# Tying weight sums two steps back, and moving a spilled operand's stores to another DMA queue, in a one-core hybrid decoder layer

## The chip, the cores and the metric

The kernel runs on one core of a Trainium2 chip. The metric is the device time of one execution in microseconds, median of several runs. Engines are named as the profile names them: PE is the matrix engine (TensorE), PEld its weight loads, DVE is VectorE, ACT is ScalarE, POOL is GpSimd, SP is SyncE, which here only issues DMAs. Each engine takes its instructions in order and waits at an instruction until the semaphores it names are reached.

## The reference

One decoder layer over 1040 positions (16 learned tokens and 1024 of input), width 1024, everything in float32:

```
u = rmsnorm(h);  z = u @ w_in            -> q, k, v, x_rec, y_rec
A = gelu(y_rec) * rg_lru(conv4(x_rec));  B = sliding-window attention with sinks
h = h + rmsnorm(concat(B, A) @ w_out)
h = h + rmsnorm(square(relu(rmsnorm(h) @ w_ff1)) @ w_ff2)
```

The change lies in the last line, the feed-forward part: a product of 1024x1024 by 1024x4096 and one of 1024x4096 by 4096x1024.

## The kernel before

Products of float32 are made of three matmuls of float32r: each operand is split into a high part (a copy with a cast to float32r, on ACT, line 96) and a low part (source minus high part, on DVE, line 99), and `mm3` (lines 125, 126, 127) adds high x high, high x low and low x high into one bank. Where the text says "low part" of a weight tile it means the line-99 subtraction.

Both feed-forward products are done by a scheme of Strassen's kind: the matrices are cut in two by two blocks, and seven products of sums of blocks replace eight. That makes sums: `combine` (line 989) is one DVE addition or subtraction, and some sums of weight blocks are left to the DMA engines (`accum_op=ADD`, line 1258, from POOL's queue: the first block is loaded by SP, and the second is added to it in place).

**First product.** One of the sums of the activations, T4, is needed late. Its two operand pairs (high and low part of each half of the contraction) are made early in `t_rest` (from line 1163), stored to `t4_dram` by four DMAs of 512 KB (line 1165; the trace calls it t_dram), and read back into `ot4` by four DMAs some 130 us later (line 1217). Four other tiles of weight sums per round are kept the same way: `prep_a` stores each to `s_dram` (line 1034, POOL's queue), and the tile that it leaves is refilled by a weight load. `product` runs through four blocks of the contraction, three matmuls each; the first of the products with T4 is written otherwise, in `product_by_parts`: four matmuls of high x high, then four of low weight x high operand, then four of high weight x low operand, so that T4's low parts are needed last.

**Second product.** A list of 56 steps, seven products (i) times eight pieces (q) of the contraction, at 24 matmuls a step. `fetch_2(n)` loads the weight block or blocks of step n into the two `raw` and two `e` buffers, `prep_2(n)` sums them where a sum is DVE's, splits them into one of four `ws` buffers, and makes the activation side. In products 1 and 2 (steps 8 to 23) the sum of two weight blocks is an accumulating DMA where q % 3 < 2, and a DVE `combine` in steps 10, 13, 18 and 21; in products 3, 4 and 6 it is DVE's more often. A `raw` or `e` buffer is free for a later step's load when its low part or its `combine` is done.

The order of each engine's instructions is not that of the source. A scheduler with a timeline model places them, and `behind(name, ins)` adds a constraint to it without a semaphore: `ins` goes behind the named instruction. In the last product (i == 6) the weight sum is held behind the low part of the step before:

```
ins = combine(raws[0], raws[0], raws[1], wx[2])
if i == 6:
    behind(w_low[0], ins)
```

Of the kernel before, what the change touches and what calls it, by code (L numbers as in the profile page):

```python
# [37 lines left out]
def hybrid_layer(  # L38
# [6 lines left out]
    nc = tc.nc  # L45
# [12 lines left out]
    def slot(tag, shape, dt=F32):  # L58
        uid[0] += 1
        return slab.tile(shape, dt, tag=tag, name=f"{tag}{uid[0]}", bufs=bufs[tag])  # L60

    def pair(tag, shape):
        return slot(tag, shape, F32R), slot(tag, shape, F32R)

    def bank(tag, shape=(P, 512)):
        uid[0] += 1
        return ps.tile(list(shape), F32, tag=tag, name=f"ps_{tag}{uid[0]}")

    def f32(ap):
        return ap.bitcast(F32)  # L70
# [23 lines left out]
    def split(hi, lo, src, eng=None):  # L94
        if eng is None:
            nc.scalar.copy(hi, src)  # L96
        else:
            eng.tensor_copy(hi, src)
        low = nc.vector.tensor_tensor(lo, src, f32(hi), op=ALU.subtract).ins  # L99
        mark[0] = low.name  # L100
        return low
# [4 lines left out]
    def behind(name, *inss):  # L106
        for ins in inss:
            tc.add_manual_dep(
                ins, name,
                mybir.DependencyInfo(  # L110
                    mybir.DependencyClass.NoSync, mybir.DependencyReason.DATA
                ),
                reason="order",
            )
# [8 lines left out]
    def mm3(dst, lhs, rhs, start, stop):  # L123
        (lh, ll), (rh, rl) = lhs, rhs
        nc.tensor.matmul(dst, lh, rh, start=start, stop=False, skip_group_check=True)  # L125
        nc.tensor.matmul(dst, lh, rl, start=False, stop=False, skip_group_check=True)  # L126
        last_mm[0] = nc.tensor.matmul(  # L127
            dst, ll, rh, start=False, stop=stop, skip_group_check=True
        ).ins.name
# [363 lines left out]
    for b in range(4):  # L493
# [3 lines left out]
        if b == 0:  # L497

            acc = [bank("acc"), bank("acc")]
# [11 lines left out]
            for w, (t0, n), sink, tag in (  # L511
                (wq, (16, 256), sink_q0, "o"), (wx, piece, sink_x0, "acc"),
            ):
                acc = bank(tag)
# [395 lines left out]
    t4_dram = dpool.tile([P, 2, 4, 512], F32, name="t4_dram")  # L910
# [77 lines left out]
    def combine(dst, x0, x1, op):  # L988
        return nc.vector.tensor_tensor(dst, x0, x1, op=op).ins  # L989
# [9 lines left out]
    def product(acc, w, op, first):  # L999
        wh, wl = w  # L1000
        for kc in range(4):
            hh, ll = op[kc // 2]
            mm3(
                acc, (wh[:, kc, :], wl[:, kc, :]), (hh[:, kc % 2, :], ll[:, kc % 2, :]),
                first and kc == 0, kc == 3,
            )
# [50 lines left out]
    def fetch_c(p):  # L1057
        r1 = slot(("e", "raw")[third.index(p) % 2], [P, 4, 256])
        w1_load(r1, 1, p, 0, 2)
        return r1  # L1060

    def prep_c(p):
        r1 = raw_c.pop(p)
        hi, lo = pair("ws", [P, 4, 256])
        split(hi, lo, r1)
        return (hi[:, :, LO], lo[:, :, LO]), (hi[:, :, HI], lo[:, :, HI])
# [8 lines left out]
    def block(k, p):  # L1075
        q = p // 2
        if fb[k][q] is None:
            fb[k][q] = slot(FTAG[k][q], [P, 2, 512])
        return fb[k][q][:, p % 2, :]

    def activate(k, q):
        t_ = fb[k][q]
        nc.scalar.activation(t_, t_, AF.Relu)
        return nc.scalar.activation(t_, t_, AF.Square).ins
# [20 lines left out]
    for t in range(8):  # L1105
# [12 lines left out]
        if t == 6:  # L1118
            b21 = operand(u2f[0][2:4])
            hl = slot("b", ESH, F32R), slot("e", ESH, F32R)  # L1120
# [33 lines left out]
    def t_rest(k):  # L1154
        i = k % 2
        if k < 2:
            behind(mark[0], combine(u2f[1][i], u2f[1][i], u2f[0][i], ALU.subtract))
        elif k < 4:
            behind(mark[0], combine(t2[i], u2f[0][2 + i], t2[i], ALU.subtract))
        else:  # L1160
            hl = pair("a", [P, 2, 512])
            late = mark[0]
            behind(late, split(*hl, t2[i]))
            for n in range(2):
                nc.sync.dma_start(t4_dram[:, n, 2 * i : 2 * i + 2, :], f32(hl[n]))

    raw_b, raw_c = {}, {}
    for p in range(16):
        if p + 2 < 16:
            wa[p + 2] = prep_a(p + 2, None if p else urgent)  # L1170
        if p >= 13:
            raw_b[p - 13] = fetch_b(p - 13)
        product(ya[p], wa[p][1], ot2, False)
        nc.scalar.copy(block("12", p), ya[p])
        if 4 <= p + 2 < 16:
            p1(p + 2, wa[p + 2][0])
        product(ya[p], wa[p][2], ot3, False)
        nc.scalar.copy(block("21", p), ya[p])
        if 3 <= p < 9:
            t_rest(p - 3)  # L1180

        if p == 14:
            ot1 = operand(u2f[1][0:2])
# [13 lines left out]
    for p in range(16):  # L1197
# [7 lines left out]
        if p == 15:  # L1205
            wc = {third[0]: prep_c(third[0])}
# [5 lines left out]
        if p == 2:  # L1212
            ob21 = operand(u2f[0][2:4])
    ot4 = [pair("b", [P, 2, 512]) for _ in range(2)]
    for n in range(2):
        for i in range(2):
            nc.sync.dma_start(f32(ot4[i][n]), t4_dram[:, n, 2 * i : 2 * i + 2, :])

    def product_by_parts(acc, w, op):
        for k, (a, b) in enumerate(((0, 0), (1, 0), (0, 1))):  # L1220
            for kc in range(4):
                nc.tensor.matmul(
                    acc, w[a][:, kc, :], op[kc // 2][b][:, kc % 2, :],
                    start=k == 0 and kc == 0, stop=k == 2 and kc == 3,
                    skip_group_check=True,
                )

# [19 lines left out]
    def fetch_2(n):  # L1249
        i, q = steps[n]  # L1250
        wx = PLAN[i][1]
        tags = (("raw", "e"), ("e", "raw"))[n % 2] if i < 6 else LASTW[q]
        raws = []
        for (a, b), tag in zip(wx[:2], tags):
            if len(wx) == 3 and wx[2] is ADD and raws and (
                q % 3 < 2 if i < 6 else tag is None
            ):
                nc.gpsimd.dma_start(raws[0], w2v[q, a, b], accum_op=ADD)
                break
            r = slot(tag, [P, 2, 512])  # L1260
            nc.sync.dma_start(r, w2v[q, a, b])
            raws.append(r)
        return raws

    def prep_2(n, tag="ws"):
        i, q = steps[n]
        fx, wx, _ = PLAN[i]
        raws = raw_2.pop(n)
        if len(raws) == 2:
            ins = combine(raws[0], raws[0], raws[1], wx[2])  # L1270
            if i == 6:
                behind(w_low[0], ins)
        wh, wl = pair(tag, [P, 2, 512])
        w_low[0] = split(wh, wl, raws[0]).name
        if len(fx) == 3:
            f = slot("b", [P, 2, 512])
            combine(f, fb[fx[0]][q], fb[fx[1]][q], fx[2])
        else:
            f = fb[fx[0]][q]
        fh, fl = pair("b", [P, 2, 512])  # L1280
        split(fh, fl, f)
        return fh, fl, wh, wl
# [2 lines left out]
    steps = [(i, q) for i in range(7) for q in range(8)]  # L1285
    ready, raw_2 = {}, {}

    w_low = [None]

    load_root(squared)  # L1290

# [2 lines left out]
    for n, p in enumerate(third):  # L1294
        if n + 2 < 16:
            raw_c[third[n + 2]] = fetch_c(third[n + 2])
        if n >= 13:
            raw_2[n - 13] = fetch_2(n - 13)
        if n + 1 < 16:
            wc[third[n + 1]] = prep_c(third[n + 1])  # L1300
        if n == 15:
            ready[0] = prep_2(0)
        if p not in a12_early:
            y2 = bank(("acc", "s")[p % 2])
            product(y2, wc[p][0], ob21, True)
            nc.vector.tensor_tensor(block("11", p), y2, block("11", p), op=ALU.add)
        y4 = bank(("pt", "o")[p % 2])
        if n == 0:
            product_by_parts(y4, wc[p][1], ot4)
        else:  # L1310
            product(y4, wc[p][1], ot4, True)
        nc.vector.tensor_tensor(block("21", p), y4, block("21", p), op=ALU.add)
        done.add(p)
        if p ^ 1 in done:
            activate("11", p // 2)
            activate("21", p // 2)
# [183 lines left out]
```

## Time and profile before

| | us |
|---|---|
| median of 3 runs | 957.42 (956.74 to 957.98) |
| the profiled execution, own time | 957.43 |
| its span in the trace | 955.7 |
| PE busy in the span | 944.6 |
| DVE, ACT, POOL busy | 659.3, 504.3, 124.6 |

The span is counted from the first to the last instruction of the trace; 1.7 us of the execution lie outside it. A line of a timeline has start and length in us, engine, source line, operation and tiles, how many were merged, and in brackets how long the engine sat idle before it and what ended that. Buffer numbers are left out, so which step a `raw`, `e` or `ws` belongs to is told in the text. A line of the waits has total time, number of times and the longest. The granted TensorE clock is 1.0 throughout. Loads and casts that are named below by step were put to their steps by the order of the instructions in the built program.

### The profile page before, as it was taken

Reading aid. Unit: us, or ns where it says so; the run is one execution under the profiler, and the core shown is the slowest. Engines: PE = TensorE matmul, PEld = TensorE weight load, DVE = VectorE, ACT = ScalarE, POOL = GpSimd, SP = SyncE. Lnnn points to the kernel's source line nnn. Section 1 sums busy time; section 2 is a strip of 40 time slices with the busy share of each in tenths; the row PEclk is TensorE's granted clock in tenths of the full one; section 3 lists DMA queues with packets and bytes.
Section 4 is the critical chain, followed back from the end, with each engine's and each line's share of the span. In section 5 each row is a group of like instructions: output and inputs, shape, how many; then the busy total and the mean of one; then the engine's idle time right before and its main releaser. Section 6 shows DMA issues by size and latency. Waiting matters only on the chain.

```text
span 955.7 us, 12406 instructions
## 1 busy us (share of the span) xinstructions
PE 944.6 (99%) x4728; PEld 789.8 (83%) x4728; DVE 659.3 (69%) x845; ACT 504.3 (53%) x854; POOL 124.6 (13%) x184
## 2 busy tenths in 40 slices
PE   9999999999999999999999999999999999999996
PEld 8999999877888877888888878888888788888885
DVE  6567997779866776665644465476576776779883
ACT  7537766478645554443555575563433343446441
POOL 4102563420020100000000000000111100001201
PEclk9999999999999999999999999999999999999999
DMA  8221011104235466675522353324767765547934
GB/s 271 57 67 23 24 45 46 45 23 134 77 120 177 133 220 198 197 259 160 184 102 90 110 192 119 109 92 129 176 171 182 198 219 178 197 133 199 241 67 89
DMA packets 88200, 130.22 MB, mean 136 GB/s; under 512 B 13702, under 2 KB 52630, under 8 KB 88140
## 3 DMA queue, kind: packets, MB, share of 16 engines
q1 hardware_dynamic: 79548, 106.54, 34.3%
q0 software_dynamic: 8160, 21.57, 10.9%
q10 hardware_dynamic: 432, 1.31, 0.4%
q8 instruction: 37, 0.61, 0.3%
q14 instruction: 23, 0.19, 0.1%
HBM read 109.93 MB, written 18.87 MB: 135 GB/s over the span
## 4 chain that ended last, share of the span: by engine, by line
PE 91%; DVE 3%; ACT 2%; SPq 1%; POOL 1%; DMA 1%; issue 1%; DVEq 0%; ACTq 0%; POOLq 0%
PE ps_acc L125 11%; PE ps_acc L126 11%; PE ps_acc L127 11%; PE ps_pt L125 7%; PE ps_pt L126 7%; PE ps_pt L127 6%; PE ps_s L127 6%; PE ps_s L126 6%; PE ps_s L125 6%; PE ps_o L127 5%; PE ps_o L126 5%; PE ps_o L125 5%; PE ps_o L684 1%; POOL c L673 1%; ACT c L82 1%; DMA c<-in_x_dram 1%
## 5 line engine op out<-in xcount | busy, mean ns | idle before, releaser
L96 ACT CAST ws<-raw 128x1024 fp32r<-128x1024 f32 (+1 forms) x68 | 69.6, 1024 | 121.6 <-PE ps_o L126 46.9
L99 DVE TENSOR_TENSOR ws<-raw,ws 128x1024 fp32r<-128x1024 f32 (+1 forms) x69 | 82.4, 1195 | 53.8 <-ACT ws L96 52.8
L125 PE MATMUL ps_acc<-a,ws 128*128 128x256 f32 (+2 forms) x256 | 85.8, 335 | 0.0
L127 PE MATMUL ps_acc<-a,ws 128*128 128x256 f32 (+2 forms) x256 | 85.2, 333 | 0.0
L126 PE MATMUL ps_acc<-a,ws 128*128 128x256 f32 (+2 forms) x256 | 85.1, 333 | 0.0
L99 DVE TENSOR_TENSOR b<-b,b 128x1024 fp32r<-128x1024 f32 (+2 forms) x50 | 58.9, 1179 | 25.9 <-PE ps_o L126 17.1
L96 ACT CAST ws<-e 128x1024 fp32r<-128x1024 f32 x41 | 42.9, 1046 | 64.0 <-PE ps_o L126 40.2
L96 ACT CAST b<-b 128x1024 fp32r<-128x1024 f32 (+2 forms) x49 | 50.0, 1019 | 45.8 <-DVE b L989 40.2
L99 DVE TENSOR_TENSOR ws<-e,ws 128x1024 fp32r<-128x1024 f32 x41 | 50.1, 1223 | 24.2 <-ACT ws L96 24.0
L673 POOL TENSOR_SCALAR_AFFINE_SELECT c<-c 128x512 fp32r<-128x512 f32 x64 | 52.1, 834 | 70.3 <-ACT c L96 60.8
L125 PEld LDWEIGHTS ps_acc<-a,ws 128*128 128x128 f32 x256 | 48.3, 189 | 4.6 <-issue 0.2
L127 PEld LDWEIGHTS ps_acc<-a,ws 128*128 128x128 f32 x256 | 48.2, 188 | 4.5
L126 PEld LDWEIGHTS ps_acc<-a,ws 128*128 128x128 f32 x256 | 48.1, 188 | 4.4 <-issue 0.4
L126 PE MATMUL ps_acc<-ws,b 128*128 128x512 f32 (+1 forms) x120 | 46.2, 385 | 0.9 <-DVE ws L99 0.9
L125 PE MATMUL ps_acc<-ws,b 128*128 128x512 f32 (+1 forms) x120 | 46.2, 386 | 0.0
L127 PE MATMUL ps_acc<-ws,b 128*128 128x512 f32 (+1 forms) x120 | 46.2, 385 | 0.0
L125 PE MATMUL ps_pt<-ws,b 128*128 128x512 f32 x112 | 44.4, 396 | 0.0
L126 PE MATMUL ps_pt<-ws,b 128*128 128x512 f32 x112 | 44.1, 394 | 0.0
L127 PE MATMUL ps_pt<-ws,b 128*128 128x512 f32 x112 | 44.0, 393 | 0.0
L125 PE MATMUL ps_s<-ws,b 128*128 128x512 f32 x110 | 43.4, 395 | 0.0
L127 PE MATMUL ps_s<-ws,b 128*128 128x512 f32 x110 | 43.3, 394 | 0.0
L126 PE MATMUL ps_s<-ws,b 128*128 128x512 f32 x110 | 43.3, 393 | 0.0
(414 smaller groups left out, 2662.7 us busy)
## 6 DMA issues: line engine op xcount, KB each, us to landing
raw<-in_w_ff_dram SPq DMA_DIRECT2D x61, 512.0 KB, 4.4
e<-in_w_ff_dram SPq DMA_DIRECT2D x45, 512.0 KB, 3.4
d<-in_w_ff_dram SPq DMA_DIRECT2D x12, 512.0 KB
s_dram<-d POOLq DMA_DIRECT2D x12, 512.0 KB, 4.1
c<-in_x_dram SPq DMA_DIRECT2D x8, 512.0 KB, 3.5
raw<-in_w_in_dram SPq DMA_DIRECT2D x8, 512.0 KB
d<-in_x_dram SPq DMA_DIRECT2D x8, 512.0 KB, 3.2
out_dram<-raw SPq DMA_DIRECT2D x8, 512.0 KB
```

What stands on the lines that cost most here:

```text
L82: ins = nc.scalar.activation(*args, **kwargs).ins
L96: nc.scalar.copy(hi, src)
L99: low = nc.vector.tensor_tensor(lo, src, f32(hi), op=ALU.subtract).ins
L125: nc.tensor.matmul(dst, lh, rh, start=start, stop=False, skip_group_check=True)
L126: nc.tensor.matmul(dst, lh, rl, start=False, stop=False, skip_group_check=True)
L127: last_mm[0] = nc.tensor.matmul(dst, ll, rh, start=False, stop=stop, skip_group_check=True).ins.name
L673: nc.gpsimd.affine_select(out=p_[:, :, s], in_=f32(p_[:, :, 0]), pattern=[[0, 4], [g, P]], compare_op=op, fill=0.0, base=0, channel_multip ...
L684: nc.tensor.matmul(po[:, oc : oc + n], v, p_[:, pc : pc + n], start=first and k == 0, stop=last and k == 1, skip_group_check=True,)
```

## The change

Three things, in one diff:

- the four stores of T4 are issued on POOL's queue, not SP's;
- the four loads that bring it back come as high and low part of the first half of the contraction, then of the second half (before: both high parts, then both low parts), and the first product with T4 uses the ordinary `product`, block by block, in place of `product_by_parts`;
- a DVE sum of weight blocks of step n goes behind the low part of step n - 2 (in products before the last).

```diff
-                nc.sync.dma_start(t4_dram[:, n, 2 * i : 2 * i + 2, :], f32(hl[n]))
+                nc.gpsimd.dma_start(t4_dram[:, n, 2 * i : 2 * i + 2, :], f32(hl[n]))
...
     ot4 = [pair("b", [P, 2, 512]) for _ in range(2)]
-    for n in range(2):
-        for i in range(2):
+    for i in range(2):
+        for n in range(2):
             nc.sync.dma_start(f32(ot4[i][n]), t4_dram[:, n, 2 * i : 2 * i + 2, :])
-
-    def product_by_parts(acc, w, op):
-        for k, (a, b) in enumerate(((0, 0), (1, 0), (0, 1))):
-            for kc in range(4):
-                nc.tensor.matmul(
-                    acc, w[a][:, kc, :], op[kc // 2][b][:, kc % 2, :],
-                    start=k == 0 and kc == 0, stop=k == 2 and kc == 3,
-                    skip_group_check=True,
-                )
...
             if i == 6:
                 behind(w_low[0], ins)
+            elif n > 1:
+                behind(w_lows[n - 2], ins)
         wh, wl = pair(tag, [P, 2, 512])
-        w_low[0] = split(wh, wl, raws[0]).name
+        w_low[0] = w_lows[n] = split(wh, wl, raws[0]).name
...
-    w_low = [None]
+    w_low, w_lows = [None], {}
...
-        if n == 0:
-            product_by_parts(y4, wc[p][1], ot4)
-        else:
-            product(y4, wc[p][1], ot4, True)
+        product(y4, wc[p][1], ot4, True)
```

In the built program the number of instructions of each engine is the same but for the four DMA issues that pass from SP to POOL. DVE's order differs in five places: the weight sums of steps 10, 13, 18, 21 and 24 now stand behind the low parts of steps 8, 11, 16, 19 and 22. With that the order of SP's loads and of POOL's accumulating DMAs differs as well: step 12 comes ahead of 11, 15 ahead of 14, 20 ahead of 19, and 23 ahead of 22.

## The prediction

> **What bounds the kernel now.** I read the page's busy times first, then the busy times by stage, then PE's waits, and then the timelines around the two waits that are left in the stages of the change.
>
> ```profile
> PE 944.6 (99%) x4728; PEld 789.8 (83%) x4728; DVE 659.3 (69%) x845; ACT 504.3 (53%) x854; POOL 124.6 (13%) x184
> ...
> 365.00:640.00 275.00, 275.00 (x1186) 222.50 (x1185) 156.15 (x183) 146.62 (x168) 6.41 (x12) 1.00 0.46 150
> 640.00:950.00 310.00, 307.42 (x1373) 250.93 (x1371) 225.22 (x220) 132.36 (x174) 26.95 (x24) 1.00 0.61 167
> ...
> PE ps_acc L126 <- DVE ws L99: 0.9, 1, 0.9
> ...
> PEld ps_pt L1222 <- DMA b<-t_dram: 0.4, 1, 0.4
> ```
>
> In the second and third row the figures behind the stage and its length are the busy times of PE, PEld, DVE, ACT and POOL. PE is busy for 99% of the span, and the change touches the stages from 365 us on alone. There PE waits twice that the waits show: once for a weight's low part (0.9 us) and once, at its weight load, for the T4 operand (0.4 us). Those two places, and what the change puts in their stead, decide. First T4:
>
> ```profile
> 557.16 0.40 PE L125 MATMUL ps_o<-b,ws 128*128 128x512 f32 x1
> ...
> 559.71 0.39 PE L127 MATMUL ps_o<-b,ws 128*128 128x512 f32 x1
> 559.94 3.21 PE L1222 MATMUL ps_pt<-b,ws 128*128 128x512 f32 x12
> 562.99 0.39 PE L125 MATMUL ps_s<-b,ws 128*128 128x512 f32 x1
> ...
> 562.41 0.30 PEld L1222 LDWEIGHTS ps_pt<-b,ws 128*128 128x128 f32 x2 [0.43 <-DMA b<-t_dram]
> ...
> 552.95 2.85 SPq L1217 DMA_DIRECT2D b<-t_dram  x4
> ```
>
> Twelve matmuls of one block take (559.71 - 557.16)/11 = 0.231 us each; the row at 559.71 is the twelfth. Twelve of T4's first product should take 2.78 us and take 562.99 - 559.94 = 3.05: this stall costs 0.27. Matmul 11 (due 559.94 + 10 x 0.231 = 562.25) is the first to use the last of the four loads, so that load lands at about 562.4. The four are issued between 552.95 and 555.8.
>
> **The reads by halves.** The built program gives the four loads the same places and the same releases in turn (a free pair, then the other), so I keep the landings: the fourth at 562.4 whichever part it is. In block order matmul 7 is the first to use the second half's high part and matmul 8, due 559.94 + 7 x 0.231 = 561.56, the second half's low part: the fourth load. It waits 562.4 - 561.56 = 0.85 us, plus what a restart costs. For that the row of the other stall, quoted below: its first matmul behind the wait takes 0.50 in place of 0.39, so 0.1. The stall becomes 0.95 in place of 0.27: **+0.7**. The bounds are -0.3 (the halves land in time after all, and the old stall goes) and +0.7; I take +0.7, as nothing in the change makes a load earlier.
>
> **The stores.** They leave SP, where each took 0.34 us to issue, and stand between POOL's stores to s_dram.
>
> ```profile
> 350.77 0.55 POOL L1034 DMA_DIRECT2D s_dram<-d  x1 [16.45 <-DVE d L989]
> 351.37 0.53 POOL L1034 DMA_DIRECT2D s_dram<-a  x1
> ...
> 408.32 0.53 POOL L1034 DMA_DIRECT2D s_dram<-d  x1 [6.09 <-DVE d L989]
> 416.68 0.53 POOL L1034 DMA_DIRECT2D s_dram<-d  x1 [7.82 <-DVE d L989]
> ...
> 415.01 0.34 SPq L1165 DMA_DIRECT2D t_dram<-a  x1
> 419.03 0.37 SPq L986 DMA_DIRECT2D raw<-in_w_ff_dram  x1
> 420.16 0.34 SPq L1165 DMA_DIRECT2D t_dram<-a  x1
> 420.59 0.39 SPq L986 DMA_DIRECT2D d<-in_w_ff_dram  x1
> ...
> 426.72 0.68 DVE L99 TENSOR_TENSOR e<-raw,e 128x512 fp32r<-128x512 f32 x1
> ...
> 429.21 0.40 PE L125 MATMUL ps_s<-b,e 128*128 128x512 f32 x1
> ```
>
> POOL is idle 6 to 8 us ahead of each store to s_dram, and two stores were issued 0.6 apart at 350.77, so a second in flight does not hold the queue. The new one at 415.01 will be issued by 415.6, before the store at 416.68. Queued behind that on POOL is nothing but the next stores; who waits for them is SP's reload of the `d` tile (420.59), and behind that DVE's sum and the low part at 426.72, which ends at 427.40 and is read at 429.21: 1.8 us of room. On SP the loads behind the stores gain at most 0.34 each. The reads of T4 come 130 us later. Cost: **0**, bounds 0 and, should the store at 416.68 be held until its neighbour has landed, some 2 us late, +0.2 beyond that room. A rule speaks against this edit: the Trainium skill's page "DMA: Bandwidth & Descriptors", section "Queues, rings and completion order", says that one queue's descriptors are consumed in ring order on each DMA engine while different queues take turns, so two stores that shared the engines from two queues would now stand in line. By that rule too the sum stays the same, since the line is shorter than the 1.8 us; no row before shows such a pair on one queue.
>
> **The sum of weights behind the low part.** Around the other wait:
>
> ```profile
> 735.31 1.05 ACT L96 CAST ws<-e 128x1024 fp32r<-128x1024 f32 x1 [1.98 <-PE ps_o L126]
> ...
> 736.52 1.22 DVE L989 TENSOR_TENSOR b<-b,c 128x1024 f32<-128x1024 f32 x1
> 740.51 1.23 DVE L989 TENSOR_TENSOR e<-e,raw 128x1024 f32<-128x1024 f32 x1 [2.77 <-DMA raw<-in_w_ff_dram]
> 741.65 1.22 DVE L99 TENSOR_TENSOR ws<-e,ws 128x1024 fp32r<-128x1024 f32 x1
> ...
> 741.59 0.40 PE L125 MATMUL ps_o<-ws,b 128*128 128x512 f32 x1
> 742.93 0.50 PE L126 MATMUL ps_acc<-ws,b 128*128 128x512 f32 x1 [0.94 <-DVE ws L99]
> ```
>
> The low part at 741.65 is step 19's. Its cast ended at 736.4, but DVE first had to do step 21's weight sum, which waited until 740.5 for its load. PE lost 742.93 - 741.59 - 0.23 + 0.1 = 1.2. Behind the change the low part goes first and needs only step 19's weights; the sum is **-1.2** if these are there.
>
> **What comes with it.** The new places in DVE's order free the buffers in another order, and POOL's accumulating DMAs follow: steps 12 and 11, 15 and 14, 20 and 19, 23 and 22 change places. POOL's issues (the pairs stand at 680.57, 698.91, 726.33, 745.81):
>
> ```profile
> 680.57 1.20 POOL L1258 DMA_DIRECT2D e<-in_w_ff_dram  x1 [11.29 <-DMA e<-in_w_ff_dram]
> 686.33 1.22 POOL L1258 DMA_DIRECT2D raw<-in_w_ff_dram  x1 [4.56 <-DVE b L989]
> 698.91 1.21 POOL L1258 DMA_DIRECT2D raw<-in_w_ff_dram  x1 [11.37 <-DVE b L99]
> 704.71 1.21 POOL L1258 DMA_DIRECT2D e<-in_w_ff_dram  x1 [4.59 <-DVE b L989]
> 712.62 1.21 POOL L1258 DMA_DIRECT2D raw<-in_w_ff_dram  x1 [6.70 <-issue]
> ...
> 726.33 1.21 POOL L1258 DMA_DIRECT2D e<-in_w_ff_dram  x1 [6.47 <-DMA e<-in_w_ff_dram]
> 732.03 1.21 POOL L1258 DMA_DIRECT2D raw<-in_w_ff_dram  x1 [4.50 <-DVE b L99]
> 745.81 1.21 POOL L1258 DMA_DIRECT2D raw<-in_w_ff_dram  x1 [12.57 <-DVE b L989]
> 752.75 1.21 POOL L1258 DMA_DIRECT2D e<-in_w_ff_dram  x1 [5.73 <-issue]
> ...
> raw<-in_w_ff_dram POOLq DMA_DIRECT2D x6, 512.0 KB, 5.8
> ...
> 714.07 0.39 PE L126 MATMUL ps_acc<-ws,b 128*128 128x512 f32 x1
> ...
> 759.76 0.39 PE L126 MATMUL ps_acc<-ws,b 128*128 128x512 f32 x1
> ...
> 741.77 0.37 SPq L1261 DMA_DIRECT2D raw<-in_w_ff_dram  x1
> ```
>
> Within a pair the second is issued 5.7 to 6.9 after the first, as long as one takes to land (5.8): one accumulation at a time. So steps 11, 14, 19 and 22, each wanted first, get their weights a slot later. From a landing to the end of the low part it is a cast (1.05), a subtraction (1.23) and 0.1: 2.4. Step 14: issue 704.71 + 5.8 + 2.4 = 712.9; PE reads it at 714.07, so 1.2 to spare. Step 19: 732.03 + 5.8 + 2.4 = 740.2, wanted at 741.59 + 0.23 = 741.82: 1.6 to spare, and the -1.2 stands. Step 22: step 23's load is now freed by that low part, 740.2; load to accumulation is 745.81 - 741.77 = 4.0, so 744.2; this pair's own spacing 6.9 gives 751.1 for step 22; + 5.8 + 2.4 = 759.3. PE reads it at 759.76 - 1.2 = 758.55: late by 0.75, with restart **+0.8**. With a spacing of 5.7 it is in time: bounds 0 and +0.8 (more in the second rival). I take +0.8, by the pair's own row.
>
> **The sum**, against the profiled execution's own 957.43 (the median is 957.42): +0.7 + 0 - 1.2 + 0.8 = +0.3: **957.7 us**.
>
> **Rivals.** *Both stalls go and nothing takes their place.* For it: the whole idle time of PE in these stages is 0.27 + 1.2 = 1.5, and step 22 may be in time. Against it: the fourth T4 load has to land 0.85 earlier than now. Time 957.43 - 1.5 = 955.9.
>
> *The late slot feeds itself: slower.* It decides at step 14. The slot that step 14 takes over, from 704.71, lasted until 712.62, 7.9 and not 5.8. If it does again, the weights land at 712.3, the low part ends at 714.7 and PE stalls 0.7. Step 18's load waits for that buffer, falls into the running accumulation of step 16, and lengthens it; at a spacing of 6.9 in place of 5.8 for four accumulations (16, 17, 20, 19), less the 1.6 us in which POOL has nothing between 712.62 + 2 x 6 = 724.7 and 726.33, step 19's is issued 2.8 later, at 734.8. Its low part ends at 734.8 + 5.8 + 2.4 = 743.0, wanted at 742.5, or a microsecond later at a spacing of 6.9: of the -1.2 some 0.75 is lost. Step 23's load at 743.3 gives an accumulation at 747.3, step 22's at 754.2, its low part at 762.4, wanted at 759.76 + 0.7 + 0.75 - 1.2 = 760.0: 2.4 and restart. Sum 0.7 + 0.7 - 1.2 + 0.75 + 2.5 = +3.5: 960.9. For it: the very slot was 7.9 long, and loads that share the engines stretched it. Against it: the other three slots before were 5.7 to 6.9.
>
> *The change doesn't do what it says*: the tie takes no hold, because step 19's weights land after step 21's. Then the -1.2 stays out and only +0.7 counts: 958.1. Against it: 1.6 us to spare at step 19.
>
> **How the numbers follow.** The forecast has 0.40, the self-feeding slot 0.40, both stalls gone 0.12, no hold 0.05, anything faster 0.03 (it would need more than the 1.5 us that PE idles). 0.2% of 957.42 is 1.9 us, about what a measurement of this kernel can tell from no change: 955.5 and 959.3 are the limits. Forecast, both stalls gone and no hold lie within: 0.57; slower 0.40; faster 0.03. The range goes from 955.9 to the rival's 961.0. The forecast's own range is 956.9 (step 22 in time) to 959.
>
> **What would show it.** Right: the first product with T4 has a gap of 0.85 at its eighth matmul; no wait of PE near 741; a wait of some 0.7 for a line-99 low part near 758; POOL's pairs still 5.7 to 7 apart. The slower rival shows a first new wait near 713 and a larger one near 760. Wrong: T4's fourth load landing by 561.5; a wait of PE between 420 and 470, which would be the stores'; any new wait behind 770, where I count none.

## The result: 1% slower, and the profile after

The changed kernel takes 967.54 us (966.66 to 969.58, 4 runs), the kernel before in the same comparison 957.36 (956.74 to 957.98): a ratio of 1.0109, 95% interval 1.0092 to 1.0127. The forecast was 957.7 with a range to 961.0, so the time lies 6.5 us outside it. The profiled execution took 967.81 us, with a span of 966.1; against 957.43 and 955.7 before that is 10.4 us more.

The page's busy times hardly tell it:

```profile
PE 949.1 (98%) x4728; PEld 791.3 (82%) x4728; DVE 659.0 (68%) x845; ACT 503.8 (52%) x854; POOL 127.7 (13%) x188
```

PE's share falls by one point and its busy time rises by 4.5 us, although it does the same matmuls: some of them took longer. Next, PE's waits behind 360 us (total, times, longest):

```profile
PE ps_acc L125 <- ACT ws L96: 6.1, 3, 2.5
PE ps_pt L126 <- DMA b<-t_dram: 1.3, 2, 0.8
```

The one wait for a low part is gone, and the T4 wait has become two. New are three waits, 6.1 us together, of a step's first matmul for the cast of its weight. PE's timeline shows where they are, each as the last row ahead of the wait and the first behind it:

```profile
559.88 0.40 PE L125 MATMUL ps_pt<-b,ws 128*128 128x512 f32 x1
560.77 0.50 PE L126 MATMUL ps_pt<-b,ws 128*128 128x512 f32 x1 [0.49 <-DMA b<-t_dram]
...
562.08 0.50 PE L125 MATMUL ps_pt<-b,ws 128*128 128x512 f32 x1
563.38 0.50 PE L126 MATMUL ps_pt<-b,ws 128*128 128x512 f32 x1 [0.81 <-DMA b<-t_dram]
...
714.70 0.40 PE L127 MATMUL ps_o<-ws,b 128*128 128x512 f32 x1
716.42 0.50 PE L125 MATMUL ps_acc<-ws,b 128*128 128x512 f32 x1 [1.32 <-ACT ws L96]
...
744.47 0.40 PE L127 MATMUL ps_o<-ws,b 128*128 128x512 f32 x1
747.14 0.50 PE L125 MATMUL ps_acc<-ws,b 128*128 128x512 f32 x1 [2.28 <-ACT ws L96]
747.48 0.44 PE L125 MATMUL ps_s<-ws,b 128*128 128x512 f32 x1
747.71 0.63 PE L125 MATMUL ps_pt<-ws,b 128*128 128x512 f32 x1
748.14 0.63 PE L125 MATMUL ps_o<-ws,b 128*128 128x512 f32 x1
...
765.24 0.40 PE L127 MATMUL ps_o<-ws,b 128*128 128x512 f32 x1
768.10 0.76 PE L125 MATMUL ps_acc<-ws,b 128*128 128x512 f32 x1 [2.46 <-ACT ws L96]
```

They are the first matmuls of steps 14, 19 and 22. The rows at 747.71 and 748.14 start 0.43 apart, not 0.23: PE is at half clock. The busy times by window show that too (behind the window and its length: PE, PEld, DVE, ACT, POOL, the granted clock, the DMA share, GB/s):

```profile
744.27:747.69 3.42, 1.14 (x5) 0.64 (x4) 0.57 (x1) 1.65 (x2) 0.00 (x0) 1.00 0.03 5
747.69:751.10 3.41, 3.41 (x9) 2.50 (x8) 3.41 (x4) 1.29 (x2) 0.00 (x0) 0.50 0.43 138
751.10:754.50 3.40, 3.40 (x16) 2.75 (x15) 2.46 (x4) 1.20 (x2) 1.20 (x1) 1.00 0.59 174
764.76:768.17 3.41, 0.95 (x5) 0.45 (x3) 0.09 (x1) 1.17 (x2) 0.00 (x0) 1.00 0.04 7
768.17:771.58 3.41, 3.41 (x8) 2.69 (x9) 3.41 (x4) 2.72 (x3) 0.00 (x0) 0.50 0.28 103
```

For 3.41 us behind each of the two longest waits the clock is 0.50. A stretch of 3.41 us at 0.427 us a matmul instead of 0.231 loses 3.41 x (1 - 0.231/0.427) = 1.6 us.

The account, from each matmul's start set against the same matmul before: T4 +1.7; step 14 +1.8; step 19 +2.5 for the wait, -1.2 for the old wait that is gone, +1.6 for the clock; step 22 +2.6 and +1.6. The sum is 10.6; PE's last matmul starts 10.7 later.

### The profile page after: what moved, and what is told of

Its sections match the earlier page's. It is cut to its first block, busy times and chain, and to the rows that moved or that the text cites. A ratio compares the mean times of both kernels' runs of the same rounds, so it can differ in the third digit from the quotient of the medians.

```text
span 966.1 us, 12414 instructions
## 1 busy us (share of the span) xinstructions
PE 949.1 (98%) x4728; PEld 791.3 (82%) x4728; DVE 659.0 (68%) x845; ACT 503.8 (52%) x854; POOL 127.7 (13%) x188
## 4 chain that ended last, share of the span: by engine, by line
PE 86%; DMA 5%; DVE 4%; issue 2%; ACT 2%; POOL 1%; DVEq 0%; POOLq 0%; SPq 0%; ACTq 0%
PE ps_acc L125 10%; PE ps_acc L126 10%; PE ps_acc L127 10%; PE ps_pt L126 6%; PE ps_pt L125 6%; PE ps_pt L127 6%; PE ps_s L127 6%; PE ps_s L125 6%; PE ps_s L126 6%; PE ps_o L125 5%; PE ps_o L126 5%; PE ps_o L127 5%; DMA e<-in_w_ff_dram 2%; DMA raw<-in_w_ff_dram 2%; PE ps_acc L276 1%
## 5 line engine op out<-in xcount | busy, mean ns | idle before, releaser
L125 PE MATMUL ps_acc<-ws,b 128*128 128x512 f32 (+1 forms) x120 | 47.2, 395 | 6.1 <-ACT ws L96 6.1
L126 PE MATMUL ps_acc<-ws,b 128*128 128x512 f32 (+1 forms) x120 | 47.1, 393 | 0.1
L127 PE MATMUL ps_acc<-ws,b 128*128 128x512 f32 (+1 forms) x120 | 46.8, 390 | 0.0
```

Of the source, the lines that this page charges most:

```text
L127: last_mm[0] = nc.tensor.matmul(dst, ll, rh, start=False, stop=stop, skip_group_check=True).ins.name
```

## The experiments

Two questions: which part costs what, and why. My theories were that the order of the accumulating DMAs, not the tie itself, makes the three waits, and that something in the order of T4's four loads makes them late.

**The tie alone**, the stores and the reads as before:

```diff
+            elif n > 1:
+                behind(w_lows[n - 2], ins)
```

> The tie alone: the weight sum of step n behind the low part of step n - 2; T4's stores and reads as before. Theory (the late slot feeds itself): the accumulations of steps 11, 14, 19 and 22 stay second in their pairs, so PE waits 1.5 to 2 us at step 14, about 2.5 at step 19 and about 2.7 at step 22, and two of the waits are followed by some 3.4 us at half the granted clock; without T4's +1.7 the whole is +8.5 to +9.5 us, 966 to 967. Rival (the three parts act on one another: the later T4 shifts the loads against the accumulations): the tie alone gives no more than the +0.3 less 0.7 of the prediction, about 957, at most +2.

967.22 us against 957.97, ratio 1.0108 (1.0092 to 1.0125). Its profiled execution took 963.87. PE's waits behind 360 us:

```profile
PE ps_acc L125 <- ACT ws L96: 5.6, 3, 2.7
PE ps_s L127 <- DVE ws L99: 0.2, 1, 0.2
```

The same three waits: against before, +1.0 at step 14, +2.7 at step 19 (-0.8 of the old one), +3.2 at step 22; the last matmul is 6.3 late. The tie makes them, without the other two parts. In this one profile the clock did not fall; its mean granted clock was 0.998, those of the other four runs (965.6 to 970.5 us) 0.994 to 0.996. Those four kept no trace, so that the clock fell in them is read from the mean alone.

**The tie with the DMAs held in step order.** `in_order` puts each SP load and each accumulation of the second product behind the one of the step before it, up to step 24:

```diff
+    def in_order(e, dma, n):
+        if fetch_last[e] and n < 25:
+            behind(fetch_last[e], dma.ins)
+        fetch_last[e] = dma.ins.name
```

> The tie as in the change, and the weight loads of SP and the accumulations of POOL held in step order up to step 24. Theory (the order of the accumulations is the cause, not the tie): no wait at steps 14, 19 and 22, the old wait of 1.2 us at step 19 gone, full clock throughout: 956.2, that is -1.2. Rival (a weight sum that comes later frees its buffers too late whatever the order of the DMAs): waits of a microsecond or more at steps 14 and 22 stay, 959 or more.

957.24 us, ratio 0.9994 (0.9978 to 1.001); I had put it at 956.2. All three waits are gone and the old one near 741 too: PE gains 1.2 us there against the trace before, and is 1.7 earlier at the end. DVE's order keeps the tie. POOL's issues of the last three pairs, each with the step that is wanted first ahead, as in the kernel before:

```profile
698.53 1.21 POOL L1265 DMA_DIRECT2D raw<-in_w_ff_dram  x1 [9.48 <-DVE b L989]
705.73 1.21 POOL L1265 DMA_DIRECT2D e<-in_w_ff_dram  x1 [5.99 <-ACT b L96]
...
727.43 1.21 POOL L1265 DMA_DIRECT2D e<-in_w_ff_dram  x1 [7.18 <-ACT b L96]
736.15 1.21 POOL L1265 DMA_DIRECT2D raw<-in_w_ff_dram  x1 [7.51 <-issue]
744.40 1.21 POOL L1265 DMA_DIRECT2D raw<-in_w_ff_dram  x1 [7.05 <-DVE ws L99]
752.82 1.21 POOL L1265 DMA_DIRECT2D e<-in_w_ff_dram  x1 [7.21 <-issue]
```

The slots are long here too (7.2, 8.7 and 8.4 us from the first of a pair to the second), and PE waits for none of them: a long slot costs only where the step that is wanted first stands behind it. So the exchanged order of the DMAs is the cause; SP's loads and POOL's accumulations were held together, and which of the two orders matters more was not separated.

**The stores alone.**

```diff
-                nc.sync.dma_start(t4_dram[:, n, 2 * i : 2 * i + 2, :], f32(hl[n]))
+                nc.gpsimd.dma_start(t4_dram[:, n, 2 * i : 2 * i + 2, :], f32(hl[n]))
```

> Only the four stores of T4 on GpSimd's queue. Theory (the stores cost nothing): same as before within 0.3 us, and the four loads of T4 land as before, the last near 562.4 by the trace's time. Rival (the stores' queue makes T4's loads come later, which would explain why they landed 1 us later behind the change): the last load lands near 563.3 and the first product with T4 waits 1.2 us in place of 0.3: +1.

959.38 us, ratio 1.0014 (1.0002 to 1.0025), while in its trace PE is 0.4 earlier at the end than before, waits for no store, and the old wait near 741 stays (1.1 us). The later pair on one chip (below, 958.33 with the stores on POOL and 958.31 without) shows no cost. By the spread of its runs (955.5 to 962.8) I estimate that it would miss one below 1.5 us, so the 1.4 of the first comparison is neither found in a trace nor excluded.

**The reads by halves alone**, with the ordinary product:

```diff
-    for n in range(2):
-        for i in range(2):
+    for i in range(2):
+        for n in range(2):
...
-            product_by_parts(y4, wc[p][1], ot4)
+            product(y4, wc[p][1], ot4, True)
```

> Only the reads of T4 by halves, and the ordinary product in place of the one by parts; stores on SP, no tie. Theory (the fourth load lands when it did, and is needed three matmuls earlier): one wait of 0.85 us at the eighth matmul, +0.7. Rival (the order of the loads itself makes them land later, as behind the change): waits of 0.65 and 1.1 us at the second and eighth matmul, +1.7.

962.38 us, ratio 1.0044 (1.0032 to 1.0056). PE's waits:

```profile
PE ps_pt L125 <- DMA b<-t_dram: 1.3, 1, 1.3
PE ps_pt L126 <- DMA b<-t_dram: 1.1, 2, 0.8
```

Three waits, and behind them a phase of half clock. The loads are issued when they were before, from 552.9 us on, and yet land later: the fourth at 564.5, before at 562.4.

**Which tie starts it.** Three kernels tie only some of the sums (21; 10 and 13; 18 and 21); the rest of the DMA order stays as before. The edit, for the first of them:

```diff
-            elif n > 1:
+            elif n == 21:
                 behind(w_lows[n - 2], ins)
```

> Only the sum of step 21 is held behind step 19's low part; of the accumulations only steps 23 and 22 change places, the pairs 12/11, 15/14 and 20/19 stay as in the kernel before. If the delay at step 22 is handed down from the late slots at 14 and 19 (a chain): no wait at step 14, the old wait near 741 gone (-1.2), at step 22 none or some 0.8: about 957 us, 0.5 to 1.2 below the kernel before. If the exchange of 23 and 22 costs by itself what the trace of the change shows there (2.7 to 2.9): 957.9 - 1.2 + 2.8 = 959.5, and 961 with one phase of half clock (1.7).

With step 21 alone (23 ahead of 22): 959.03 us against 957.85, ratio 1.0013 (1.0 to 1.0027). In the trace, of one of the faster executions (957.56), the old wait is gone and step 22 loses 0.3 behind its late slot. The trace sides with the chain, the median is nearer to the rival's 959.5 than to my 957, so this run alone does not decide.

> Only the sums of steps 10 and 13 are tied: the accumulations go 12, 11 and 15, 14, but 19, 20 and 22, 23 as in the kernel before. Theory (the late slot of step 14 hands its delay on, and only a step that again stands second in its pair feels it): a wait of 0.7 to 1.5 at step 14, none above 0.8 at step 22, the old wait near 741 still there at 1.1 to 2: 958.9 to 960. Rival (the first exchange alone sets the whole train late): waits above 2 at 19 and at 22 as with the whole tie: 962 to 967.

With 10 and 13 (12 ahead of 11, 15 ahead of 14): 961.6 us against 957.84, ratio 1.0032 (1.0015 to 1.0048). One wait of 3.3 us at step 14 with a half clock behind it, and none at 19 or 22. POOL's issues around it, step 15's and step 14's:

```profile
700.68 1.21 POOL L1258 DMA_DIRECT2D e<-in_w_ff_dram  x1 [12.93 <-DVE b L989]
709.49 1.21 POOL L1258 DMA_DIRECT2D raw<-in_w_ff_dram  x1 [7.61 <-DVE b L99]
```

Step 14 comes second, and it is issued 8.8 us behind the first of the pair and not 5.8. The wait itself I had put at 0.7 to 1.5; that the later pairs, in their old order, do not feel it was as expected. The old wait near 741, which I had expected to stay, is not there, although the sum of step 21 is not tied (more on this below).

> Only the sums of steps 18 and 21 are tied: the accumulations go 20, 19 and 23, 22, but 11, 12 and 14, 15 as in the kernel before. Theory (chain from step 14): no wait at step 14, step 19's weights come one undisturbed slot late and just in time, the old wait goes (-1.1), at step 22 0 to 1.5: 957 to 958.5. Rival (each exchange costs by itself what it cost with the whole tie): waits of 2.7 near 742 and of 2.9 near 762, and about 962 to 966.

With 18 and 21 (20 ahead of 19, 23 ahead of 22): 964.55 us, ratio 1.006 (1.0039 to 1.0082). My theory here was wrong. Step 14 is in time, and still PE waits at both later places:

```profile
734.91 1.21 POOL L1258 DMA_DIRECT2D e<-in_w_ff_dram  x1 [4.76 <-DVE b L989]
...
735.81 0.37 SPq L1261 DMA_DIRECT2D raw<-in_w_ff_dram  x1
...
743.16 1.05 ACT L96 CAST ws<-e 128x1024 fp32r<-128x1024 f32 x1 [7.38 <-DMA e<-in_w_ff_dram]
...
744.26 0.50 PE L125 MATMUL ps_acc<-ws,b 128*128 128x512 f32 x1 [0.76 <-ACT ws L96]
...
764.39 0.50 PE L125 MATMUL ps_acc<-ws,b 128*128 128x512 f32 x1 [2.80 <-ACT ws L96]
```

Step 19's accumulation is issued at 734.91, an SP load falls in 0.9 behind it, and the cast that waits for it starts at 743.16: 8.25 us for a way that I had put at 5.8. So a chain is there, but a shorter one than I thought: an exchange needs no late step ahead of it to cost. That a late step ahead makes it dearer fits the traces (against before, step 19 starts 1.0 later here and 2.7 with the whole tie; step 22 loses 3.0 here and 0.3 with step 21's tie alone), but these are single executions.

**What sets a slot's length.** All 16 profiles hold 12 such accumulations each, in the steps to 23. By how much SP's queue moved between the issue and the last packet: up to 250 KB, 46 of them, 5.1 to 5.6 us; over 600 KB, 60 of them, 5.7 to 8.2, median 7.2. A longer slot also has more time to count loads in; counted over the first 5 us of each slot alone, the 42 with under 150 KB took 5.2 to 5.6 us and the 20 with over 600 KB 6.4 to 8.0. So the length goes with the loads beside it; no run took a load away on its own, so for the single slot it is read from the trace, not shown by a kernel.

**Why T4's loads land late.** In `t4_dram` the parts lie as [n, i], so the old order of loads takes a 16 KB row at 0, 4, 8 and 12 KB, the new one at 0, 8, 4 and 12. Two kernels store the parts as [i, n]: one with the new order of loads, which now rises through the row, one with the old order, which now jumps.

```diff
-    t4_dram = dpool.tile([P, 2, 4, 512], F32, name="t4_dram")
+    t4_dram = dpool.tile([P, 2, 2, 2, 512], F32, name="t4_dram")
...
-            nc.sync.dma_start(f32(ot4[i][n]), t4_dram[:, n, 2 * i : 2 * i + 2, :])
+            nc.sync.dma_start(f32(ot4[i][n]), t4_dram[:, i, n, :, :])
```

> The reads by halves alone, but with the halves' parts stored next to each other, so that the four loads in their new order again take the bytes of a row in rising order (0, 4, 8, 12 KB in place of 0, 8, 4, 12). If the order of the addresses slowed the loads: the fourth lands at about 562.4 again, the only wait is some 0.9 at matmul 8, and the time is 957.9 + 0.7 = 958.6, some 3.8 below the run with the halves alone (962.4). If the destinations, or what PE does meanwhile, slowed them: landings to 564.5, waits of 3 us and about 962.

959.05 us, ratio 1.0007 (0.9994 to 1.0019), against 1.0044 with the same reads in the old layout. One T4 wait is left:

```profile
562.79 0.50 PE L126 MATMUL ps_pt<-b,ws 128*128 128x512 f32 x1 [0.85 <-DMA b<-t_dram]
```

> The kernel before with T4's rows stored in the other layout, and nothing else: each engine's instructions are the same, but the four loads take the bytes of a row in the order 0, 8, 4, 12 KB. If the order of the addresses slows them: the fourth lands at 563.3 to 564.5 in place of 562.4, the wait at the first product with T4 grows from 0.3 to 1.2 or 2.4, and the time is 959 to 962. If it is something else in the order by halves: no difference, 957.9.

959.54 us, ratio 1.0023 (1.001 to 1.0035); every engine's instructions are those of the kernel before. The first product with T4:

```profile
565.07 2.14 PE L1222 MATMUL ps_pt<-b,ws 128*128 128x512 f32 x8 [0.78 <-DMA b<-t_dram]
567.65 0.73 PE L1222 MATMUL ps_pt<-b,ws 128*128 128x512 f32 x2 [0.44 <-DMA b<-t_dram]
```

Two waits in place of one; T4 costs 1.5 us more than before. The time proves less than the landings: this trace (961.87) also lost 4.0 us near 449, a fall of the clock among it, and it has no old wait near 741. From the issue of the first load to the last packet of the fourth: 8.7 to 9.9 us in the eleven profiles whose loads rise through the row, 10.0 to 11.2 in the five whose loads jump; a packet of 4 KB took 0.184 to 0.198 us on average in the first and 0.206 to 0.216 in the second. All four combinations of layout and order are among them: old layout rising (the kernel before) and jumping (the halves), new layout rising and jumping (these two). So the order of the addresses does it, with either product and either order of parts. By what mechanism, no run here tells.

**Whole changes with the order held.**

> The whole change, with the loads and accumulations of the second product held in the order of the steps. If the exchanged order is all that the tie costs, the waits at 14, 19 and 22 go and those at the first product with T4 stay: 957.9 + 1.8 (T4) - 1.3 (old wait) = 958.4, up to 962 with phases of half clock behind the T4 waits, as in the run with the halves alone (962.4). If the stores on GpSimd's queue or the halves also bear on the second product, waits near 714, 744 or 765 come back: above 963.

With `in_order` alone: 959.87 us, ratio 1.0016 (1.0002 to 1.003); in the trace two T4 waits (2.0 us together) and none at 14, 19 or 22.

> The whole change with the order of the accumulations held and the halves' parts stored next to each other. If the exchanged order and the order of the addresses are the two causes, no wait of PE at 14, 19 or 22, one of 0.9 at matmul 8 of T4's first product, no phase of half clock: 957.9 + 0.9 - 1.2 = 957.6, against 967.5 for the change as it is. If a third thing is in it: above 960.

With `in_order` and the layout: 957.79 us against 957.84, ratio 1.0002 (0.999 to 1.0014); its trace has the one T4 wait of 0.8 us, none at 14, 19 or 22, and one near 449 that was not forecast (below). Within some 1.2 us the two causes hold the whole 10 us.

**The clock again**: the changed kernel itself, once more.

> The changed kernel once more, for where its clock drops. If the clock is judged in steps of 3.413 us on a grid that is fixed within an execution, each phase of half clock begins a whole number of 3.413 after the others (the one behind the last matmul too), and follows a step in which PE idled 2.0 us or more, whatever the length of the single wait: a wait of 2.7 or 2.9 that straddles a border of the grid leaves the clock full. If it is the length of a wait alone, each of the waits near 744 and 765 drops it. 964 with no drop, 965.7 with one, 967.5 with two.

967.79 us. The waits came out otherwise, and with them the clock:

```profile
744.63:748.04 3.41, 1.64 (x8) 0.99 (x6) 0.00 (x0) 0.91 (x1) 0.00 (x0) 1.00 0.37 67
748.04:751.45 3.41, 3.15 (x13) 2.29 (x13) 3.24 (x4) 2.05 (x3) 0.00 (x0) 1.00 0.25 70
765.11:768.52 3.41, 1.18 (x5) 0.67 (x4) 0.81 (x1) 1.89 (x2) 0.00 (x0) 1.00 0.13 23
768.52:771.93 3.41, 3.41 (x9) 2.36 (x8) 3.41 (x4) 2.00 (x3) 0.00 (x0) 0.50 0.49 169
```

One fall of the clock, not two: behind the window in which PE began five matmuls (2.4 us idle), none behind the one with eight (1.9 us). The time I had given for one fall was 965.7; instead PE is 3.7 us late ahead of step 14, against 1.8 in the first profile: 2.6 of it at T4, 0.9 ahead of T4.

**Does the good part alone gain?** The tie in step order, with the stores on POOL and without:

> The tie with the accumulations held in order, and T4's stores on GpSimd's queue; the reads as before. If the stores cost nothing: as the run without them, 957.2, no wait of PE at 14, 19 and 22 and at T4's first product 0.3 to 0.9. If the stores cost the 1.4 that the runs of the stores alone gave (959.4 against 958.0): 958.6, and a wait or slower transfers between 400 and 470.

> The tie with the accumulations held in order once more (957.2 against 958.0 in the first runs, the interval on both sides of 1): whether the 1.1 us that PE no longer waits near 741 is a gain. If it is: ratio 0.998 to 0.999. If other stretches take it back in most executions: 0.999 to 1.001.

958.33 and 958.31 us against 958.65, ratios 0.9989 (0.9973 to 1.0005) and 0.9995 (0.9979 to 1.0012). The old wait is gone in both traces, and both intervals hold 1. In their profiles PE waits 1.9 and 0.5 us near 449, where the profile before has no wait; in some of the other profiles it is up to 2.3, with the stores on either queue. The second kernel's instructions up to there are those of the kernel before, so this differs from execution to execution, and may hide the gain.

There may be a second reason why no gain shows. Six of the traced kernels do not tie step 21. The old wait is in the traces of two of them (before 0.9 us, the stores alone 1.1), and not in those of four (the halves alone, the two kernels that change only the layout or the layout and the halves, and steps 10 and 13 tied). In the two, DVE idles 2.8 and 3.0 us at step 21's sum until its load lands; in the four 0.3 to 0.5. Those four leave the tie nothing to gain; why that load is there in time in them, no run tells. No version measurably beats the kernel before.

## Why the prediction was wrong

**The reads by halves, +0.7: wrong landings.** The step that failed is "I keep the landings" and, with it, +0.7 as the upper bound: nothing made a load earlier, but the order of the addresses made all four land 1.0 to 1.5 us later, at the same issue times. Measured +1.7 in the whole change, and 4.5 with the half clock in the kernel with the halves alone. The arithmetic behind it was right: in the layout in which the loads keep their pace there is one wait, of 0.85 us, at matmul 8, the number forecast. The wait at matmul 2, for the second load, I had not looked at, since with the old landings it had 0.9 to spare.

**The stores, 0: right as far as it was measured.** No wait of PE between 420 and 470 in the trace after, and 958.33 against 958.31. The sign named against it, a wait between 420 and 470, is in other traces (near 449), but with the stores on either queue. The store to s_dram that follows a T4 store on POOL's queue by 1.3 us, at 416.43 in the trace after, landed 3.6 us behind its issue, the one at 416.68 before in 3.4. The Trainium skill's rule on ring order that the prediction set against the stores gave the same sum, and these rows show no delay that mattered. (The prediction says that no row before shows two stores in a row on one queue; its own rows at 350.77 and 351.37 are such a pair.)

**The sum behind the low part, -1.2: right mechanism, but not a sure gain.** The kernel with step 21 tied alone shows it:

```profile
738.36 1.22 DVE L99 TENSOR_TENSOR ws<-e,ws 128x1024 fp32r<-128x1024 f32 x1
...
741.10 1.22 DVE L989 TENSOR_TENSOR e<-e,raw 128x1024 f32<-128x1024 f32 x1 [0.93 <-DMA raw<-in_w_ff_dram]
```

Step 21's sum still waits for its load, and step 19's low part no longer stands behind it. But the old wait is missing in four traces without the tie as well (above), so the -1.2 is the gain against the one profile that the prediction was worked from.

**What comes with it, +0.8: the step that failed.** I had the four exchanged pairs, and that the second of each pair comes a slot late; I sized the slot at 5.7 to 5.8 (6.9 for the last pair), and left the start of the pairs where it was. POOL's issues after, the last three pairs:

```profile
701.46 1.20 POOL L1249 DMA_DIRECT2D e<-in_w_ff_dram  x1 [11.89 <-DVE b L989]
709.18 1.22 POOL L1249 DMA_DIRECT2D raw<-in_w_ff_dram  x1 [6.53 <-issue]
...
731.32 1.20 POOL L1249 DMA_DIRECT2D raw<-in_w_ff_dram  x1 [8.62 <-DMA raw<-in_w_ff_dram]
739.02 1.22 POOL L1249 DMA_DIRECT2D e<-in_w_ff_dram  x1 [6.51 <-issue]
752.45 1.20 POOL L1249 DMA_DIRECT2D e<-in_w_ff_dram  x1 [12.21 <-DVE b L989]
759.48 1.22 POOL L1249 DMA_DIRECT2D raw<-in_w_ff_dram  x1 [5.82 <-issue]
```

The spacings are 7.7, 7.7 and 7.0. With the prediction's own working, term by term (us; the starts of the pairs are set against PE, which is itself 1.8, 3.8 and 6.7 late ahead of these steps):

| | step 14 | step 19 | step 22 |
|---|---|---|---|
| room in the forecast | 1.2 | 1.6 | -0.75 |
| the pair starts later | 0.8 | 1.2 | 0.4 |
| spacing in the pair, above the forecast's | 1.9 | 2.0 | 0.1 |
| the step's own accumulation to its last packet, above 5.8 | -0.1 | 0.9 | 1.4 |
| late by | 1.4 | 2.5 | 2.6 |
| PE's wait in the trace | 1.3 | 2.3 | 2.5 |

So the mis-sized term is the slot ahead: 2 us too short at steps 14 and 19, which alone uses up the room there; at step 22 it is the step's own accumulation. A slot of 7.9 us was already in the profile before. I gave it to the rival and not to the forecast. The prediction also looked for these waits at the low part; PE stops one matmul earlier, at the cast.

**The rival "The late slot feeds itself"** had the right places (a first new wait near 713, a larger one near 760) and 0.40. Its sizes for the tie were +0.7, 0.75 lost of the -1.2, and 2.5; in the trace of the tie alone they are +1.0, 2.7 where the old wait had been, and 3.2. Step 19 is the mis-sized one: I had its accumulation at 734.8 with four slots of 6.9; two of them took 8.0 and 7.0 to their last packet, and it was issued at 737.18. It also had the long slot at step 14 in the wrong place: step 14's own accumulation took 5.7 us in the trace after, and the one of step 15 ahead of it was the long one. That step 14 must come first is not so.

**Not foreseen at all: the clock.** I called it 1.0 throughout (in the profile before it is 1.0 from 7.1 us on, and 0.5 from 952.6, behind the last matmul) and priced waits by their length. Two falls in the profiled execution are 3.2 of the 10.7 us.

## What to carry to other kernels

A scheduling hint on one engine can also move the DMAs that wait for its buffers: list the new order of every queue, and where two serialised transfers change places, price the slot by the longest one in the trace, not the mean. A move of DVE's order can often be kept while the DMAs' order is held as it was. When reads of a spilled tile are re-ordered, change the layout with them, so that they still rise through it. And a wait of PE is not worth its length alone: once most of one clock window is idle, add the slow phase behind it.

## What the runs showed of the hardware

**The clock is judged on a fixed grid.** In the profile after, the half-clock phases begin at 747.69, 768.17 and, behind the last matmul, at 962.73: 6 and 57 times 3.413 us apart. In every other trace with one, it also lies a whole number of 3.413 us from the one at the end. What counts is how much of one such window is idle, not the length of a wait. From the matmuls' starts (0.23 us a matmul, and the slower start behind a wait and gaps of one missing record not counted as idle), the idle time in the windows ahead of a fall is 1.97 to 3.30 us, and the largest without a fall 1.95. Counted with those gaps, it is 2.08 and more with a fall and up to 2.03 without. So the limit lies near 2.0 us, and no finer figure can be read from these traces. The tie alone shows best that it is not the length of a wait: its wait ahead of 764.81 is the longest in that trace, 2.9 us, and straddles a border:

```profile
760.45:763.87 3.42, 1.63 (x7) 0.96 (x6) 0.00 (x0) 0.16 (x1) 0.00 (x0) 1.00 0.79 137
763.87:767.28 3.41, 2.41 (x9) 1.71 (x10) 2.49 (x3) 3.41 (x4) 0.00 (x0) 1.00 0.08 9
767.28:770.69 3.41, 3.41 (x16) 2.75 (x16) 2.14 (x2) 0.33 (x1) 0.00 (x0) 1.00 0.87 279
```

The clock stays full. The grid's place differs between executions, and with it which waits cost 1.6 more; that goes with the spread of the timed runs of the tie alone. The Trainium skill's page "TensorE: Matmul & The Clock Gate", Part 1, section "What's actually happening", gives a free-running window of 3413 ns; these traces agree. Its section "Why this matters for your kernels" warns of idle gaps over some 3 us; here about 2.0 us within one window was enough, and in the kernel with the halves alone two waits of 1.3 and 0.8 us did it together.

**A row read out of order is slower.** The same four 512 KB loads, issued at the same pace, took about 1.5 us longer (10.0 to 11.2 us against 8.7 to 9.9) when their 4 KB pieces of a 16 KB row came as 0, 8, 4, 12 KB and not as 0, 4, 8, 12.
